# Output mix and up projection on single-bank PSUM tiles, with their sums moved from GpSimd to VectorE

## The chip, the cores and the metric

The kernel runs on one core of a Trainium2 chip. The core has a matmul engine, TensorE (PE in the profile, PEld for its weight loads), and VectorE (DVE), ScalarE (ACT), GpSimd (POOL) and SyncE (SP), each with an instruction queue of its own that it works through in order. SP only issues transfers; POOL issues some too. Matmuls write into PSUM, which has eight banks, and a tile of 128 x 512 float32 fills one bank. The metric is the time of one execution in device microseconds.

## The reference

One decoder block on a sequence of 1024 tokens, width 1024, all in float32:

```python
h = rms_norm(x, pre_norm1_w) * (1 + sc1) + sh1          # sc, sh, g from silu(c) @ w_ada
z, xbc, dt, q, k, v, gates = split(h @ w_in)
y_ssd = ssd_branch(z, xbc, dt, ...)                     # causal conv, state-space scan, gated norm
y_att = diff_attention_branch(q, k, v, ...)             # 8 heads, two softmaxes each, causal
gate_ssd, gate_att = split(sigmoid(gates))
merged = gate_ssd * (y_ssd @ w_ssd_o) + gate_att * (y_att @ w_attn_o)
mix = merged @ w_out
x = x + g1 * rms_norm(mix, post_norm1_w)
h2 = rms_norm(x, pre_norm2_w) * (1 + sc2) + sh2
u_gate, u_val = split(causal_dwconv(h2 @ w_up, conv_ffn_w, conv_ffn_b))   # D_FF = 2816 each
f = (gelu(u_gate) * u_val) @ w_down
x = x + g2 * rms_norm(f, post_norm2_w)
```

## The kernel before

**Numbers.** Every float32 operand is split into a high part (rounded by ScalarE) and a low part (VectorE: operand minus high part), and every product is three matmuls, high-high, high-low and low-high. A unit of work on PE is a 128x128 weight against 128x512. `split` (L88 to L90) is the helper, so all highs have line L89 and most lows L90.

**Stages.** In order: the conditioning rows and h (0 to 75 us from the span's start), the convolved projection xbc with twelve blocks (to 222), z (to 320), v and the state-space scan (to 497), five gate blocks "gs" (to 551), q, k and the scan's output product (to 735), attention (to 1102), its output product "ao" with eight blocks and the merge (to 1194), the passage (the output mix, the second norm, transposes, and the first two pairs of the up projection, to 1361), pairs 2 to 21 of the up projection (to 1764), the down projection (to 1986).

**Who sets the order.** From xbc on, stretches of the program fix the order of some engines by hand, in which an engine's instructions stand as they are written: in the passage and the up projection those of PE, DVE, ACT and POOL. Elsewhere a scheduler orders each queue by what is ready when, as far as it can tell. SP is always the scheduler's.

**The mix.** Eight blocks of 128 tokens; each has a PSUM tile `mix` of two banks (`ps_mm`, two such tiles in all), one bank for each half of the channels. ScalarE squares a half for the norm (`mix_square`, L1361), VectorE scales and adds (`mix_end`), PE transposes the normalized block (`first_half`, `turn`), ScalarE and VectorE make h2's parts from it. A tile is free for the block after next when its squares and scalings are done.

**The up projection** is done by Strassen's rule in Winograd's form. The 1024 rows of h2 make two halves, the tokens two halves, and a pair of channel blocks (a gate block and its value block) is taken together, so a 2x2 by 2x2 block product needs seven products of 12 matmuls each, 84 in all, in place of eight. Their order is in `order`: b11 into bank X, b21 into Z, t2 added into X, t1 into Y, t3 added into X, b22 added into Y, t4 added into X. X and Z are the two halves of one `ps_mm` tile `up`; Y has a bank of its own. Between the products, the bank as it stands is copied out by ScalarE into `evs` (L1653, L1660, L1663), and VectorE adds a bank and a copy (L1657, L1666, L1670) to make the four results `cg` and `cv`. The left operands are weight blocks and four sums of them (`up_sums`, L1269 to L1271), whose splits are made three products ahead; the convolution over tokens of the pair before (`up_conv`: ACT L1317, DVE L1318, ACT L1320, DVE L1322) is spread over the products.

**Sums for the down projection.** It uses the same rule, so it needs sums of the activations `ug` of each second pair (POOL, L1331 to L1334, stored to memory by L1336) and sums of its weights. The latter are made by `down_sums` (L406 to L418), eleven times: POOL loads two blocks of 512 KB into `wdr`, adds and subtracts four times into `wds`, and stores two blocks of 512 KB. Three of these are written into the xbc loop, eight into the z loop; two copies of one column by VectorE (L447) tie the first to block 6 of xbc.

**The first two pairs** are worked together while h2 is being transposed. Their weight sums are made by POOL and VectorE there, as are the sums and differences of h2 (`t2_sum`, `minus_b11`, and POOL's L1555 and L1557).

## Time and profile before

| | |
|---|---|
| Three runs | 1984.0, 1987.07, 1987.69 us; median 1987.07 |
| The profiled execution | 1987.92 us, of which the span is 1986.2 |
| Mean granted TensorE clock | 0.985 |
| Busy PE, DVE, ACT, POOL | 1889.3, 1212.4, 850.6, 310.1 us |
| Data moved by DMA | 301.86 MB, 152 GB/s over the span |

A row of the timeline gives the start in us from the span's start, the duration, the engine, the line, the operation, the tiles written and read, and in square brackets how long the engine stood idle before it and what released it. Matmuls overlap: a row says 0.39 us for a 128x512 matmul, and the next starts 0.23 us later when nothing waits. A row of a group gives the count, the busy time, the mean in ns, and the idle time before. A row of the waits gives the waiting engine and line, the one it waited for, and the total in us, the times and the longest.

### The profile page before, as it was taken

The numbers are of one execution on the slowest core, as the hardware profiler recorded it, in microseconds if no ns is written. First come the engines' busy times: TensorE is split into PE (matmuls) and PEld (weight loads), VectorE is DVE, ScalarE is ACT, GpSimd is POOL, SyncE is SP. The second block draws the span as 40 slices with busy tenths as digits, with TensorE's granted clock in tenths as the row PEclk, the third lists the DMA queues.
The fourth block names the chain that finished last, engine by engine and source line by source line (L and its number), as shares of the span: only waits on it lengthen the run. The fifth ranks groups of instructions, "written<-read, shape, count | busy, mean of one in ns | idle before, by whom it ended". The sixth has DMA issues, their size and how long they took to land.

```text
span 1986.2 us, 24455 instructions
## 1 busy us (share of the span) xinstructions
PE 1889.3 (95%) x9128; PEld 1563.1 (79%) x9128; DVE 1212.4 (61%) x1763; ACT 850.6 (43%) x1634; POOL 310.1 (16%) x282
## 2 busy tenths in 40 slices
PE   6999989999999999999999999888999999999998
PEld 4787988878887788888888787666777777777886
DVE  6967343565254237777766543387878887795545
ACT  5522123555222125665656422454444454555442
POOL 0005551453010000000000000141111211130001
PEclk8999999999999999999999999899999999999999
DMA  9837672133436745665632753111322322277744
GB/s 303 277 116 266 222 238 102 70 106 114 162 91 174 238 144 157 168 191 154 173 114 75 233 174 123 43 43 67 108 90 92 112 100 86 93 251 270 231 156 154
DMA packets 133132, 301.86 MB, mean 152 GB/s; under 512 B 16395, under 2 KB 47755, under 8 KB 133014
## 3 DMA queue, kind: packets, MB, share of 16 engines
q1 hardware_dynamic: 123510, 265.70, 42.2%
q0 software_dynamic: 9504, 34.61, 4.8%
q8 instruction: 72, 1.18, 0.2%
q14 instruction: 46, 0.38, 0.1%
HBM read 213.99 MB, written 86.26 MB: 151 GB/s over the span
## 4 chain that ended last, share of the span: by engine, by line
PE 77%; DVE 9%; DMA 6%; ACT 5%; issue 2%; POOL 1%; SPq 1%; POOLq 0%; DVEq 0%; ACTq 0%
PE up L1293 5%; PE up L1294 4%; PE up L1295 4%; PE o L1074 3%; PE upy L1293 2%; PE upy L1294 2%; PE upy L1295 2%; PE v L608 2%; PE v L609 2%; PE xbc L111 2%; PE v L610 2%; PE xbc L112 1%; PE at L1061 1%; PE xbc L113 1%; PE so L111 1%
## 5 line engine op out<-in xcount | busy, mean ns | idle before, releaser
L1293 PE MATMUL up<-t,wu_t 128*128 128x512 f32 x264 | 107.4, 407 | 21.8 <-ACT evs L1653 17.1
L1294 PE MATMUL up<-t,wu_t 128*128 128x512 f32 x264 | 105.2, 398 | 2.4 <-DVE t L1425 2.4
L1295 PE MATMUL up<-t,wu_t 128*128 128x512 f32 x264 | 104.7, 397 | 0.0
L89 ACT ACTIVATE wu_t<-sab 128x512 fp32r<-128x512 f32 x66 | 39.5, 627 | 126.2 <-DVE sab L1269 118.6
L1062 ACT COPY aT<-at 128x512 f32<-128x512 f32 (+2 forms) x96 | 46.1, 480 | 108.2 <-PE at L1061 108.2
L138 POOL TENSOR_TENSOR sqt<-sqt,nhalf 128x4 f32<-128x4 f32 x16 | 16.1, 1007 | 466.2 <-DVE sqt L137 466.2
L1293 PEld LDWEIGHTS up<-t,wu_t 128*128 128x128 f32 x264 | 50.7, 192 | 41.6 <-ACT evs L1653 25.6
L90 DVE TENSOR_TENSOR g_lo<-gst,g_hi 128x1024 fp32r<-128x1024 f32 (+1 forms) x42 | 48.3, 1157 | 56.3 <-ACT g_hi L89 55.9
L1074 PEld LDWEIGHTS o<-vt,aT 128*128 128x128 f32 x576 | 74.8, 191 | 9.6 <-ACT aT L1062 5.3
L90 DVE TENSOR_TENSOR wu_t<-sab,wu_t 128x512 fp32r<-128x512 f32 x66 | 47.8, 748 | 55.3 <-ACT wu_t L89 55.3
L1074 PE MATMUL o<-vt,aT 128*128 128x128 f32 x576 | 80.9, 276 | 0.2
L89 ACT ACTIVATE g_hi<-gst 128x1024 fp32r<-128x1024 f32 (+1 forms) x42 | 41.3, 989 | 74.0 <-DMA gst<-gld_s 35.7
L1331 POOL TENSOR_TENSOR gsum<-ug,ug 128x512 f32<-128x512 f32 x11 | 17.6, 1597 | 351.5 <-DVE ug L1322 351.5
L111 PE MATMUL xbc<-hT,wx_hi 128*128 128x512 f32 x160 | 64.4, 402 | 4.9 <-DVE cu L441 4.9
L1293 PE MATMUL up<-b,wu_b 128*128 128x512 f32 x176 | 68.6, 390 | 0.0
L1295 PE MATMUL up<-b,wu_b 128*128 128x512 f32 x176 | 68.5, 389 | 0.0
L1294 PE MATMUL up<-b,wu_b 128*128 128x512 f32 x176 | 68.5, 389 | 0.0
L111 PE MATMUL z<-wz_hi,hT 128*128 128x346 f32 (+1 forms) x192 | 63.1, 330 | 4.9 <-ACT wz_hi L89 4.1
L1035 DVE TENSOR_REDUCE nmx<-sc 128x1 f32<-128x640 f32 (+3 forms) x64 | 65.6, 1024 | 2.1
L112 PE MATMUL z<-wz_lo,hT 128*128 128x346 f32 (+1 forms) x192 | 63.2, 329 | 1.6 <-DVE wz_lo L90 1.6
L1356 PE MATMUL mix<-wo_hi,mT 128*128 128x512 f32 x128 | 52.7, 412 | 12.0 <-ACT tm L1361 12.0
L1015 PE MATMUL sc<-kst,qst 128*128 128x512 f32 (+2 forms) x192 | 63.7, 340 | 0.0
(429 smaller groups left out, 5950.4 us busy)
## 6 DMA issues: line engine op xcount, KB each, us to landing
wu_raw<-in_w_up SPq DMA_DIRECT2D x43, 512.0 KB, 3.5
adas<-in_w_ada SPq DMA_DIRECT2D x32, 512.0 KB, 5.0
wdr<-in_w_down POOLq DMA_DIRECT2D x22, 512.0 KB, 6.6
wtd<-wds POOLq DMA_DIRECT2D x22, 512.0 KB, 4.5
gld_s<-gsum POOLq DMA_DIRECT2D x22, 512.0 KB, 3.8
gst<-gld_s SPq DMA_DIRECT2D x20, 512.0 KB, 5.1
wdt_raw<-wtd SPq DMA_DIRECT2D x20, 512.0 KB, 4.3
gld_a<-ug SPq DMA_DIRECT2D x33, 256.0 KB, 2.0
```

Of the source, the lines that this page charges most:

```text
L89: A.activation(hi, raw, AF.Copy)
L90: V.tensor_tensor(lo, raw, hi.bitcast(F32), op=ALU.subtract)
L111: T.matmul(ps, lh, rh, start=(i == 0), stop=False)
L112: T.matmul(ps, lh, rl, start=False, stop=False)
L1015: T.matmul(sc[:, n0:n1], qs_[s][:, tsl], ks_[s][:, n0:n1], start=True, stop=False)
L1035: V.reduce_max(nmx[:, bq, s : s + 1], sc[:, :L], axis=AX.X, negate=True)
L1062: A.copy(at[:, :nk].rearrange("p k q -> p (k q)"), ptr[:, : nk * P])
L1074: T.matmul(po_of[j, grp][:, qi, :], at[:, k, :], vt[j % 2][:, kt, :], start=(kt == 0), stop=(kt == i))
L1293: T.matmul(out_, wh, xh_, start=(k == 0 and first), stop=False, skip_group_check=more)
L1294: T.matmul(out_, wh, xl_, start=False, stop=False, skip_group_check=more)
L1295: T.matmul(out_, wl, xh_, start=False, stop=(k == end), skip_group_check=more)
L1356: T.matmul(o, xh_, wh, start=(k == 0), stop=False)
```

## The change

It has five parts.

1. **PSUM.** The pool of two-bank tiles is closed after attention's output product, and four tiles of one bank each (`ps_m`) take its place. A mix block takes two of them, even blocks 0 and 1, odd blocks 2 and 3; a pair of the up projection takes one for X and one for Z, pairs 0 to 3 as 0/1, 2/3, 1/3, 0/2 and then 1/3 and 0/2 in turn. A mix block's first square is written ahead of the transposes' activations that follow its first part.
2. **POOL to VectorE.** The gate sums are made by VectorE (`up_gsum`), one at a time after four successive products, and stored by SP. The sums and differences of h2 in the passage go to VectorE too.
3. **Early weight sums.** The weight sums of pairs 0, 1 and 2 are written at blocks 0, 1 and 6 of attention's output product (`early_sums`): SP loads the weights, VectorE makes four sums, POOL stores them to memory (`wsd`). The passage loads the finished sums, in the order of the list `loads`. The splits of the first pairs are written in another order, and products 0 and 1 of pair 2 stand ahead of the last product of pairs 0 and 1.
4. **Weight loads.** All raw up weights come through three tiles by `w_load`, called at fixed products.
5. **Down sums.** The two one-column copies go. Six `down_sums` are written into the z loop, five into the gate blocks gs3 to gs7, with tiles taken anew there.

The diff, cut to its core:

```diff
+    pairs_of_banks = ExitStack()
+    pmm = pairs_of_banks.enter_context(tc.tile_pool(name="pmm", bufs=1, space=bass.MemoryType.PSUM))
     def ps_mm(name):
-        return pp.tile([P, 2, HALF], F32, tag="mm", name=name, bufs=2)
+        return pmm.tile([P, 2, HALF], F32, tag="mm", name=name, bufs=2)
...
-            if b == 6:
-                for t_ in wdr:
-                    V.tensor_copy(t_[:, 0, 0:1], u[:, 0:1])
-            if b >= 6 and b % 2 == 0:
-                down_sums(b // 2 - 3)
...
-            if q == 0 or (q == 2 and c0 < 692 and half == 0):
+            if q == 0:
                 down_sums(n_dn)
...
+    wdr = [SL.get(f"wdr{i}", F32, (P, 2, HALF)) for i in range(2)]
+    wds = [SL.get(f"wds{i}", F32, (P, 2, HALF)) for i in range(2)]
     for j in range(3, 8):
+        down_sums(n_dn)
+        n_dn += 1
         w = load_block(a["w_gate"][j], f"wgs{j}")
...
+    def early_sums(m):
+        ra, rb = [wp.tile([P, 2, HALF], F32, tag="wraw", name=f"ws{m}_{i}", bufs=3) for i in range(2)]
+        for r_, b in ((ra, fbs[m]), (rb, NFF + fbs[m])):
+            SP.dma_start(r_.rearrange("p h c -> p (h c)"), a["w_up"][b])
+        a11, a12, a21, a22 = ra[:, 0], ra[:, 1], rb[:, 0], rb[:, 1]
+        V.tensor_tensor(a22, a21, a22, op=ALU.add)
+        V.tensor_tensor(a21, a11, a21, op=ALU.subtract)
+        V.tensor_tensor(a11, a22, a11, op=ALU.subtract)
+        V.tensor_tensor(a12, a12, a11, op=ALU.subtract)
+        for i, (x_, y_) in enumerate(((a11, a22), (a21, a12))):
+            G.dma_start(wsd[m][i][:, 0], x_)
+            G.dma_start(wsd[m][i][:, 1], y_)
...
         w = load_block(a["w_attn_o"][j], f"wao{j}")
+        if j in (0, 1, 6):
+            early_sums(j if j < 2 else 2)
...
+    pairs_of_banks.close()
+    pm = ctx.enter_context(tc.tile_pool(name="pm", bufs=1, space=bass.MemoryType.PSUM))
+    def ps_m(i, name):
+        return pm.tile([P, HALF], F32, tag=f"m{i}", name=name, bufs=1)
...
+    loads = [("f", 0), ("f", 1), ("s", 0), ("s", 1), ("q", 0), ("q", 1), ("a", 0), ("f", 2), ("s", 2), ("q", 2), ("a", 2)]
+    loads += [(n, m) for m in range(3, NPAIR) for n in ("f", "v")]
...
-    def up_banks(fb):
-        mm = ps_mm(f"up{fb}")
-        banks[fb] = {"X": mm[:, 0, :], "Z": mm[:, 1, :]}
+    def up_banks(m, x_, z_):
+        banks[m] = {"X": ps_m(x_, f"upx{m}"), "Z": ps_m(z_, f"upz{m}")}
...
-        G.tensor_tensor(s1, l21, l22, op=ALU.add)
-        G.tensor_tensor(s2, s1, l11, op=ALU.subtract)
-        G.tensor_tensor(s3, l11, l21, op=ALU.subtract)
-        G.tensor_tensor(s4, l12, s2, op=ALU.subtract)
-        for i, n in enumerate(("s12", "s34")):
-            G.dma_start(gld[n][:, k, :, :], gsum[i])
+        o, x_, y_, op = ((s1, l21, l22, ALU.add), (s2, s1, l11, ALU.subtract), (s3, l11, l21, ALU.subtract), (s4, l12, s2, ALU.subtract))[i]
+        V.tensor_tensor(o, x_, y_, op=op)
+        if i % 2:
+            SP.dma_start(gld[("s12", "s34")[i // 2]][:, k, :, :], gsum[i // 2])
...
-        pms[i] = ps_mm(f"mix{i}")
+        pms[i] = [ps_m(2 * (i % 2) + ch, f"mix{i}_{ch}") for ch in range(2)]
...
+                if n == 1:
+                    mix_square(i, 0)
                 if i in (5, 6):
                     for _ in range(1 + (i == 5 and n == 3)):
...
-                if n == 1:
-                    mix_square(i, 0)
...
-        for k in down_k:
-            G.tensor_tensor(part(hb1, k), part(tbs, k), part(hb1, k), op=ALU.subtract)
-        for k in range(KH):
-            G.tensor_tensor(part(hb2, k), part(hb2, k), part(tbs, k), op=ALU.subtract)
...
+                V.tensor_tensor(part(hb1, k - 1), part(tbs, k - 1), part(hb1, k - 1), op=ALU.subtract)
+                high("t3", k - 1, hb1)
...
+        for k in range(KH):
+            V.tensor_tensor(part(hb2, k), part(hb2, k), part(tbs, k), op=ALU.subtract)
...
+        convs = {(m, p): [(up_conv, m - 1, p)] for m in range(3, NPAIR) for p in range(5)}
+        for m in range(4, NPAIR, 2):
+            for i in range(4):
+                convs.setdefault((m + (i == 3), (4 + i) % 7), []).append((up_gsum, m - 1, i))
...
+                up_banks(m, *((0, 2) if m % 2 else (1, 3)))
```

Three places in the order of VectorE's queue. The first is the xbc loop: `cu` is the convolution of a block, `accr` and `adas` belong to the conditioning rows. Before:

```order
L441 SCALAR_TENSOR_TENSOR cu0_818<-xbc6_1125,vec_73,cu0_818 128x1023
L447 COPY wdr0_814<-cu0_818 128x1
L447 COPY wdr1_815<-cu0_818 128x1
L441 SCALAR_TENSOR_TENSOR cu0_818<-xbc6_1125,vec_73,cu0_818 128x1022
L383 SCALAR_TENSOR_TENSOR accr0_806<-adas0_808,scl_79,accr0_806 128x1024
L441 SCALAR_TENSOR_TENSOR cu0_818<-xbc6_1125,vec_73,cu0_818 128x1021
```

The two copies into `wdr`, which POOL's first load of the down weights follows, stand behind block 6's first step. Now:

```order
L445 SCALAR_TENSOR_TENSOR cu0_821<-xbc6_1128,vec_76,cu0_821 128x1023
L387 SCALAR_TENSOR_TENSOR accr0_809<-adas0_811,scl_82,accr0_809 128x1024
L445 SCALAR_TENSOR_TENSOR cu0_821<-xbc6_1128,vec_76,cu0_821 128x1022
L387 SCALAR_TENSOR_TENSOR accr0_809<-adas1_812,scl_82,accr0_809 128x1024
L445 SCALAR_TENSOR_TENSOR cu0_821<-xbc6_1128,vec_76,cu0_821 128x1021
```

They are gone; nothing on this queue stands ahead of those loads.

The second place is the end of attention: `ga7` is the last gate weight, `rsm`, `coef` and `p` are the last softmax step, `sqt` and `osb` the norm of the last heads. Before:

```order
L940 TENSOR_TENSOR ga7_lo_8485<-ga7_raw_8282,ga7_hi_8484 128x512
L1051 RECIPROCAL rsm_5308<-ssum_5306 128x2
L1052 SCALAR_TENSOR_TENSOR coef_5309<-ssum_5306,nlam_5279,rsm_5308 128x1
L1053 SCALAR_TENSOR_TENSOR p1_0_5301<-p1_1_5302,coef_5309,p1_0_5301 128x1024
L1083 TENSOR_TENSOR sqt_5311<-rsm_5308 128x4
L1084 TENSOR_TENSOR sqt_5311<-sqt_5311,sso_5310 128x4
L137 TENSOR_SCALAR sqt_5311<-sqt_5311 128x4
L1092 TENSOR_TENSOR sqt_5311<-sqt_5311,rsm_5308 128x4
L1093 TENSOR_TENSOR osb_5304<-osb_5304,sqt_5311 128x512
```

Now:

```order
L944 TENSOR_TENSOR ga7_lo_8490<-ga7_raw_8287,ga7_hi_8489 128x512
L1216 TENSOR_TENSOR ws0_1_8800<-ws0_1_8800 128x512
L1217 TENSOR_TENSOR ws0_1_8800<-ws0_0_8799,ws0_1_8800 128x512
L1055 RECIPROCAL rsm_5313<-ssum_5311 128x2
L1218 TENSOR_TENSOR ws0_0_8799<-ws0_1_8800,ws0_0_8799 128x512
L1056 SCALAR_TENSOR_TENSOR coef_5314<-ssum_5311,nlam_5284,rsm_5313 128x1
L1219 TENSOR_TENSOR ws0_0_8799<-ws0_0_8799 128x512
L1057 SCALAR_TENSOR_TENSOR p1_0_5306<-p1_1_5307,coef_5314,p1_0_5306 128x1024
L1087 TENSOR_TENSOR sqt_5316<-rsm_5313 128x4
L94 TENSOR_TENSOR wao1_lo_8873<-wao1_raw_8870,wao1_hi_8872 128x1024
L1216 TENSOR_TENSOR ws1_1_8877<-ws1_1_8877 128x512
L1217 TENSOR_TENSOR ws1_1_8877<-ws1_0_8876,ws1_1_8877 128x512
```

The weight sums of pair 0 (`ws0`) stand before and between the three operations of the softmax step; those of pair 1 (`ws1`, with `wao1_lo`) stand in the norm's chain.

The third place is a pair of the up projection whose predecessor closes two pairs: `sab` are the weight sums, `wu` the splits, `ug` the activations. Before:

```order
L1322 TENSOR_TENSOR ug1_10342<-ug1_10342,uv_10343 128x1024
L1666 TENSOR_TENSOR cv0_10208<-up5_11449,evs0_9988 128x512
L1269 TENSOR_TENSOR sab00_9879<-wu38_raw_11564 128x512
L90 TENSOR_TENSOR wu16_b21_11567<-wu16_raw_11537,wu16_b21_11567 128x512
L1670 TENSOR_TENSOR cg0_10207<-upy5_11506,evs0_9988 128x512
L1269 TENSOR_TENSOR sab00_9879<-sab00_9879,wu16_raw_11537 128x512
L90 TENSOR_TENSOR wu16_t2_11584<-sab00_9879,wu16_t2_11584 128x512
L90 TENSOR_TENSOR wu16_t1_11600<-sab00_9879,wu16_t1_11600 128x512
```

Now:

```order
L1366 TENSOR_TENSOR ug1_10456<-ug1_10456,uv_10457 128x1024
L1380 TENSOR_TENSOR gsum0_10458<-ug0_10455,ug1_10456 128x512
L1720 TENSOR_TENSOR cv0_10300<-upx8_11246,evs0_10049 128x512
L1335 TENSOR_TENSOR sab0_10453<-wuv9_11284 128x512
L1322 TENSOR_TENSOR wu9_b21_11360<-wuf9_11191,wu9_b21_11360 128x512
L1380 TENSOR_TENSOR gsum0_10458<-gsum0_10458,ug0_10455 128x512
L1724 TENSOR_TENSOR cg0_10299<-upy8_11306,evs0_10049 128x512
L1335 TENSOR_TENSOR sab0_10453<-sab0_10453,wuf9_11191 128x512
L1322 TENSOR_TENSOR wu9_t2_11379<-sab0_10453,wu9_t2_11379 128x512
L1380 TENSOR_TENSOR gsum1_10459<-ug0_10455 128x512
L1335 TENSOR_TENSOR sab1_10454<-wuf9_11191,sab0_10453 128x512
```

Where the bank sums, weight sums and low parts of a pair followed each other, a gate sum (`gsum`) now stands after each product's own work, four in all; every second pair has them.

446 lines of the change are left out of this document (235 added, 211 removed).

## Prediction

> **What bounds the kernel now.** I read the page's busy shares first, then the busy time by stage, then the waits of the matmul engine (PE), then the timeline around each of its larger waits. A line of the page:
>
> ```profile
> PE 1889.3 (95%) x9128; PEld 1563.1 (79%) x9128; DVE 1212.4 (61%) x1763; ACT 850.6 (43%) x1634; POOL 310.1 (16%) x282
> ```
>
> PE is the bound nearly everywhere, so only what makes PE wait, or slows it, can change the time. Whole stages from the output mix to the steady up projection (columns: window, its length, busy PE, PEld, DVE, ACT, POOL, granted clock, DMA share, GB/s):
>
> ```profile
> 1194.00:1302.00 108.00, 96.00 (x417) 77.49 (x416) 43.43 (x68) 38.13 (x86) 15.29 (x20) 0.95 0.20 75
> 1302.00:1361.00 59.00, 52.18 (x228) 40.58 (x226) 48.47 (x64) 29.15 (x54) 15.81 (x11) 0.94 0.10 37
> 1361.00:1442.00 81.00, 73.70 (x307) 59.16 (x308) 63.89 (x75) 38.73 (x56) 14.03 (x12) 0.96 0.29 101
> 1442.00:1523.00 81.00, 78.30 (x342) 63.55 (x341) 64.39 (x77) 38.62 (x58) 14.72 (x12) 1.00 0.28 98
> ```
>
> The first three lose most, and have the lower clocks. Who is waited for:
>
> ```profile
> ACT evs L1653 <- PE up L1295: 54.5, 18, 3.7
> ...
> PE up L1293 <- ACT evs L1653: 17.1, 20, 4.0
> ...
> PE mix L1356 <- ACT tm L1361: 12.0, 6, 4.9
> ```
>
> The first two rows are a circle: ScalarE's copy of bank X waits for PE, and then PE waits for the copy, once per pair.
>
> **The circle in the up projection.** One round of it, its neighbour 20 us earlier, and the longest:
>
> ```profile
> 1429.42 0.50 PE L1293 MATMUL up<-t,wu_t 128*128 128x512 f32 x1 [0.67 <-ACT evs L1653]
> ...
> 1448.36 0.39 PE L1295 MATMUL up<-b,wu_b 128*128 128x512 f32 x1
> 1448.79 0.58 ACT L1653 COPY evs<-up 128x512 f32<-128x512 f32 x1 [3.71 <-PE up L1295]
> ...
> 1449.42 0.50 PE L1293 MATMUL up<-t,wu_t 128*128 128x512 f32 x1 [0.68 <-ACT evs L1653]
> ...
> 1385.15 1.24 ACT L1317 ACTIVATE ug<-cg,vec 128x1024 f32<-128x1024 f32 x1 [5.54 <-POOL gsum L1333]
> ...
> 1386.91 0.80 PE L1293 MATMUL up<-t,wu_t 128*128 128x512 f32 x1 [4.01 <-ACT evs L1653]
> ```
>
> The copy needs only the first product, in X, but starts when the last matmul of the second, in Z, has ended: X and Z are halves of one tile. A pair takes 1449.42 - 1429.42 = 20.00 us. Its 84 matmuls start 0.2266 apart where nothing waits, 19.03 in all, so the circle costs 0.97 a pair, 18 times: 17.5. The wait of 4.01 has another root, POOL's gate sums in front of ScalarE. Matmuls start 0.43 apart for the next 4.9 us, so that round costs about 6.4. Pairs 2 to 21 hold 1680 matmuls, 380.7 us of 409.0 between their ends, so 28.3 are lost in all; the rest (4.4) are smaller waits in pair 2.
>
> With a tile for each bank, the copy waits for the first product alone, and has the second's 12 x 0.2266 = 2.7 us to be done in: it takes 0.58, behind at most one activation of 1.24 and one weight high part of 0.6, both queued ahead of it on ScalarE. So this wait goes, if VectorE keeps up with its new work. Its rows:
>
> ```profile
> 1372.47 1.28 DVE L1318 SCALAR_TENSOR_TENSOR uv<-cv,vec,uv 128x1023 f32<-128x1023 f32 x1
> ...
> 1373.67 0.68 DVE L1666 TENSOR_TENSOR cv<-up,evs 128x512 f32<-128x512 f32 x1
> 1374.27 0.68 DVE L1269 TENSOR_TENSOR sab<-wu_raw 128x512 f32<-128x512 f32 x1
> 1374.87 0.68 DVE L90 TENSOR_TENSOR wu_b<-wu_raw,wu_b 128x512 fp32r<-128x512 f32 x1
> ...
> 1379.25 1.22 DVE L1322 TENSOR_TENSOR ug<-ug,uv 128x1024 f32<-128x1024 f32 x1
> ...
> L90 DVE TENSOR_TENSOR wu_b<-wu_raw,wu_b 128x512 fp32r<-128x512 f32 x8 | 7.6, 956 | 0.0
> ```
>
> A pair has seven low parts, four weight sums and three bank sums, 14 operations on 128x512, and the four gate sums of every second pair add two: 16. They start 0.60 apart (1373.67, 1374.27, 1374.87) and are busy 0.68 each, so 9.6 to 10.9, with four convolution steps of 1.20 to 1.28 and the product of 1.22: 15.6 to 17.2 us of 19.03. It fits, with 2 to 3 us spare. When the circle is gone, the next to end late is the sum of bank Z and the copy (0.68, behind a low part), which nothing on PE waits for until the pair after next writes that bank; the gate sums' stores move from POOL's queue to SP's, 0.3 us of issue each, behind weight loads whose raw tiles are needed 10 us later: no cost. POOL's gate sums disappear from beside it, and with them the 0.956 mean of the last row (the same operation is 0.68 alone). I take 25.5 of the 28.3; bounds 15 (VectorE late by half a microsecond a pair) and 28.
>
> **The passage.** These rows carry it:
>
> ```profile
> 1194.27 0.69 DVE L1220 SCALAR_TENSOR_TENSOR mt<-gth,ao 128x512 f32<-128x512 f32 x1 [6.05 <-PE ao L113]
> ...
> 1261.81 0.50 PE L1356 MATMUL mix<-wo_hi,mT 128*128 128x512 f32 x1 [3.35 <-ACT tm L1361]
> ...
> 1281.87 0.79 PE L1356 MATMUL mix<-wo_hi,mT 128*128 128x512 f32 x1 [4.94 <-ACT tm L1361]
> ...
> 1311.83 0.30 PE L1418 MATMUL h2tr<-ident,xr 128*128 128x128 f32 x1 [0.89 <-DVE xr L1383]
> ...
> 1332.62 1.75 DVE L1271 TENSOR_TENSOR sab<-wu_raw,sab 128x512 f32<-128x512 f32 x1
> ...
> 1333.93 0.61 PE L1293 MATMUL up<-t,wu_t 128*128 128x512 f32 x1 [2.68 <-ACT t L1422]
> ...
> 1336.23 0.80 PE L1294 MATMUL up<-t,wu_t 128*128 128x512 f32 x1 [1.69 <-DVE t L1425]
> ```
>
> From 1194.07 to 1354.71 PE issues 552 full matmuls (125.1 us) and 64 transposes (0.0875 each, 5.6), so of 160.6 us 30.0 are lost. The mix's waits (12.0, and some 4 of half-rate matmuls after the two long ones) go: a mix block has two tiles of its own out of four, and its first square now stands ahead of the transposes' activations. Of the t waits, the part behind VectorE's 1.75 us weight sums goes, since the sums of pairs 0 to 2 come ready from memory, by five more loads of 512 KB in a stage whose DMA share is 0.20 and 0.10: they are hidden as long as SP issues them a block ahead. VectorE takes over POOL's eight subtractions of the passage, 8 x 0.6 = 5 us, in a window of 59 us where it is busy for 48, part of that being the 1.75 us slowdowns and the sums that go. What stays or is new: the change of pools makes the first mix matmul wait for both gate operations of the last block, 1.3 us from 1194.27 and about 0.4 of hand-over (1.9); the 0.89; lower waits on highs and lows of the third and last products (about 1.0 and 0.6, and 0.7 at the first); the last square, behind a weight load (0.7); transitions I can't place, 2.7. That is 8.5: gain 21.5, bounds 12 and 27.
>
> **The moved sums of the down weights.** They sit on POOL with their own loads, in before from 148 to 296 us without a break:
>
> ```profile
> 85.89 1.21 DVE L90 TENSOR_TENSOR wx_lo<-wx_raw,wx_hi 128x1024 fp32r<-128x1024 f32 x1
> ...
> 172.02 2.38 DVE L383 SCALAR_TENSOR_TENSOR accr<-adas,scl,accr 128x1024 f32<-128x1024 f32 x1 [4.09 <-DMA adas<-in_w_ada]
> ...
> 178.88 1.27 DVE L383 SCALAR_TENSOR_TENSOR accr<-adas,scl,accr 128x1024 f32<-128x1024 f32 x1
> ...
> 183.88 0.77 PE L111 MATMUL xbc<-hT,wx_hi 128*128 128x512 f32 x1 [4.93 <-DVE cu L441]
> ...
> 291.35 0.78 ACT L89 ACTIVATE wz_hi<-wz_raw 128x696 fp32r<-128x696 f32 x1 [5.16 <-DMA wz_raw<-in_w_zdt]
> ...
> 292.19 0.59 PE L111 MATMUL z<-wz_hi,hT 128*128 128x348 f32 x2 [3.66 <-ACT wz_hi L89]
> ...
> 85.00:106.00 21.00, 21.00 (x94) 17.38 (x94) 16.89 (x14) 6.53 (x8) 0.00 (x0) 1.00 0.84 290
> ...
> 120.00:148.00 28.00, 28.00 (x121) 22.50 (x120) 19.68 (x21) 8.59 (x8) 0.00 (x0) 1.00 0.29 94
> ```
>
> The loads of adas and of wz come late while POOL's loads run, and PE stops for 4.93 and 3.66 us, with half-rate matmuls behind each (some 2), and 0.9 at a low part after the second. Without their two one-column copies, six of the eleven sums can start when the tiles they reuse are free, about 75 us, and at the 13.4 us that one takes in before (11 in 148 us) they end near 155; five go to the gate blocks near 500. So both stops lose their rival: 12.0 of about 14, bounds 0 and 14. The new neighbours: from 85 to 106 the DMA engines are at 0.84 already and VectorE is busy for 16.89 of 21 us, with low parts of xbc's weights (85.89) some 2 us ahead of the block at 88 that needs the first of them (+0.5, up to 8, the price of the stop at 183.88); from 120 to 148 they are at 0.29. At 500 POOL's first rotary product queues behind the sums (+0.5, up to 2).
>
> [...]
>
> **The early sums.** Twelve operations of 0.68 and six loads and twelve stores are added at attention's end and in its output product. Those of pair 2 run beside output products; VectorE has 47 us of work in those 92 (1102 to 1194), so 2.7 more are free there. Those of pairs 0 and 1 stand, in the built order, inside the last softmax step and the last norm:
>
> ```profile
> 1082.63 0.30 PE L1061 MATMUL at<-ident,p 128*128 128x128 f32 x1 [0.95 <-DVE sqt L1083]
> ...
> 1093.77 0.32 SPq L1162 DMA_DIRECT2D stg<-atd  x1
> ...
> 1107.27 0.63 ACT L89 ACTIVATE oT<-stg 128x512 fp32r<-128x512 f32 x1 [2.31 <-DMA stg<-atd]
> ...
> 1102.00:1194.00 92.00, 89.41 (x386) 71.64 (x385) 47.11 (x66) 25.81 (x36) 0.00 (x0) 1.00 0.60 201
> ```
>
> PE already waits 0.95 for the probabilities, and two sums between reciprocal and product add 1 to 1.4. SP's stg loads stand behind weight loads that now wait for POOL's stores of the sums; at about 1097 instead of 1093.77 they make the first output products wait 2 to 3, where one already lands late (2.31). Taken: 4.5, bounds 1 and 9.
>
> **The sum**, against the profiled execution's 1987.92 us: -25.5 -21.5 -12.0 +0.5 +0.5 +4.5 = -53.5, so 1934.4. The shown median is 0.85 below that execution: 1933.6. I say **1934**.
>
> **The rivals.**
> VectorE late in each pair by half a microsecond, because its queue is in order and a low part stands behind bank sums that wait for PE: 20 x 0.5 = 10, 1944. For it: 82 to 91% busy; against: weights are prepared three products ahead. Chance 0.15.
> The hand-over at attention's end costs 14.5 instead of 4.5 (the loads late, then half-rate matmuls): 1944. Chance 0.13.
> [...] Chance 0.09.
> The copy still waits for the second product, so that only the 4.01 round and smaller waits go: 17.5 back, 1951. The separate tiles speak against it. Chance 0.03.
> On the other side, VectorE sets the pace of the up projection. Sixteen operations at the slowed row's 0.956 with the rest at 6.35 are 21.6 us a pair; with 0.4 of waits 22.0, and 20 x (22.0 - 19.03) = 59: 1993. It decides from 21.7 us a pair on (53.5 / 20 above 19.03). Against it: the slowing came from POOL, which leaves. Chance 0.06, 0.02 of it within 0.2% of before (about what a measurement of this kernel tells from no change).
> **My forecast** has 0.54: its own range is 1925 to 1943. The range of 8 in 10 reaches over the first three rivals, 1923 to 1954. So faster by over 0.2%: 0.94; within: 0.02; slower: 0.04.
>
> **What would show it.** Right: no row of PE waiting for the copy of X; pairs 19.0 to 19.3 us apart; the mix's row on the squares gone; POOL idle from 155 to 330 and no stop near 184 and 292; a new wait of about 1.9 at the first mix matmul. Wrong: pairs at 19.5 or more with a VectorE row as releaser; stops of xbc before 120; several waits of the first output products on DMA.

## The result and the profile after

The changed kernel takes **1937.87 us** (median of four runs, 1935.66 to 1939.14); the kernel before, run beside it, 1985.53 (1981.89 to 1987.69). The ratio is **0.9761**, with a 95% interval of 0.9742 to 0.9779. The profiled execution took 1938.42, its span 1936.6 us.

First the page's busy time, then rows of the list of PE's waits behind the start (what waits, for what; us in total, times, longest):

```profile
PE 1871.4 (97%) x9128; PEld 1557.7 (80%) x9128; DVE 1204.9 (62%) x1819; ACT 852.2 (44%) x1634; POOL 212.2 (11%) x214
```

```profile
PE dx L1814 <- DVE wdb_lo L94: 5.1, 1, 5.1
PE xbc L115 <- DVE cu L445: 4.8, 2, 3.6
PE upx L1344 <- ACT evs L1712: 4.8, 2, 3.5
...
PE at L1065 <- DVE sqt L1087: 2.1, 1, 2.1
...
PE mix L1402 <- DVE mt L1244: 1.5, 1, 1.5
```

The wait for the copy of X behind the first product (L1653), 20 times in before, is gone altogether. The two waits left on ScalarE's copies are for the other copy of X, the one after t1 (L1712, in before L1660, where PE waited for it once, 1.1 us); both stand in the first pairs. The wait for the squares (12.0) is gone. The longest of these waits now stands in the down projection, where no cost was expected. No row on z's weights is left. The windows (the same columns as before: window, length, busy PE, PEld, DVE, ACT, POOL, clock, DMA share, GB/s) for the mix, the first two pairs, pairs 2 to 5, steady pairs, and the start of the down projection:

```profile
1185.80:1277.30 91.50, 91.19 (x417) 75.30 (x417) 39.22 (x68) 37.35 (x86) 7.61 (x14) 1.00 0.22 79
1277.30:1337.00 59.70, 54.42 (x249) 43.35 (x247) 42.88 (x66) 32.11 (x56) 1.47 (x2) 1.00 0.26 88
1337.00:1418.00 81.00, 77.97 (x335) 64.05 (x336) 71.28 (x92) 42.88 (x63) 0.00 (x0) 0.98 0.29 101
1418.00:1499.00 81.00, 81.00 (x359) 67.07 (x358) 68.01 (x90) 39.68 (x59) 0.00 (x0) 1.00 0.31 107
1712.00:1793.00 81.00, 75.92 (x326) 62.14 (x325) 52.89 (x54) 40.99 (x51) 0.00 (x0) 0.96 0.77 258
```

In steady pairs PE is busy for the whole window: 359 matmuls in 81 us, where before had 342. One round there, from the timeline, with the same copy a pair earlier:

```profile
1448.36 0.59 ACT L1703 COPY evs<-upx 128x512 f32<-128x512 f32 x1 [0.99 <-PE upx L1346]
...
1467.20 0.39 PE L1344 MATMUL upz<-b,wu_b 128*128 128x512 f32 x1
...
1467.40 0.59 ACT L1703 COPY evs<-upx 128x512 f32<-128x512 f32 x1 [0.26 <-PE upx L1346]
```

The copy of X starts 0.2 us after Z's first matmul, not after Z's last one, and the copies stand 19.04 apart.

Where the time went, by stage, from the first matmul of each stage in the profiled executions (two experiments that are told below stand beside the two kernels; v, scan and gates reach from the last matmul of z to that of the gates, the next two stages from last matmul on):

| stage, us | before | after | banks alone | best version |
|---|---|---|---|---|
| start to z | 221.29 | 221.01 | 221.15 | 214.78 |
| z | 102.17 | 92.17 | 99.92 | 92.13 |
| v, scan, gates | 232.08 | 230.79 | 231.08 | 229.47 |
| q, k, scan's output product | 163.04 | 163.37 | 163.05 | 166.45 |
| attention | 383.65 | 385.70 | 383.49 | 383.49 |
| attention's output product | 91.84 | 92.81 | 93.14 | 88.86 |
| mix | 108.23 | 91.45 | 91.44 | 91.39 |
| up projection | 461.37 | 434.70 | 443.19 | 436.83 |
| down projection, to the end | 222.53 | 224.60 | 221.64 | 221.9 |

### The profile page after: what moved, and what is told of

It reads as the page before. It is cut to its first block, busy times and chain, and to the rows that moved or that the text cites. A ratio compares the mean times of both kernels' runs of the same rounds, so it can differ in the third digit from the quotient of the medians.

```text
span 1936.6 us, 24512 instructions
## 1 busy us (share of the span) xinstructions
PE 1871.4 (97%) x9128; PEld 1557.7 (80%) x9128; DVE 1204.9 (62%) x1819; ACT 852.2 (44%) x1634; POOL 212.2 (11%) x214
## 3 DMA queue, kind: packets, MB, share of 16 engines
q8 instruction: 72, 1.18, 0.3%
## 4 chain that ended last, share of the span: by engine, by line
PE 78%; DVE 10%; DMA 5%; ACT 4%; issue 3%; SPq 1%; POOL 0%; POOLq 0%; DVEq 0%; ACTq 0%
PE upx L1345 3%; PE upx L1346 3%; PE upx L1344 3%; PE o L1078 3%; PE dx L1814 2%; PE dx L1815 2%; PE dx L1813 2%; PE upy L1345 2%; PE upy L1346 2%; PE upy L1344 2%; PE v L606 2%; PE v L607 2%; PE dy L1815 2%; PE dy L1813 2%; PE z L116 2%
## 5 line engine op out<-in xcount | busy, mean ns | idle before, releaser
L1344 PE MATMUL upx<-t,wu_t 128*128 128x512 f32 x264 | 104.0, 394 | 4.8 <-ACT evs L1712 4.8
L1345 PE MATMUL upx<-t,wu_t 128*128 128x512 f32 x264 | 103.7, 393 | 1.9 <-DVE t L1459 1.9
L1346 PE MATMUL upx<-t,wu_t 128*128 128x512 f32 x264 | 103.2, 391 | 0.0
L1318 ACT ACTIVATE wu_t<-sab 128x512 fp32r<-128x512 f32 x57 | 34.0, 626 | 122.5 <-DVE sab L1335 122.5
L142 POOL TENSOR_TENSOR rsf<-rsf,nhalf 128x1 f32<-128x1 f32 x8 | 5.6, 703 | 639.6 <-DVE rsf L141 636.9
L115 PE MATMUL xbc<-hT,wx_hi 128*128 128x512 f32 x160 | 64.4, 402 | 4.8 <-DVE cu L445 4.8
L1344 PEld LDWEIGHTS upx<-t,wu_t 128*128 128x128 f32 x264 | 49.9, 189 | 16.6 <-ACT evs L1712 5.6
L1020 PE MATMUL sc<-klo,qst 128*128 128x512 f32 (+2 forms) x192 | 63.2, 346 | 0.0
L116 PE MATMUL xbc<-hT,wx_hi 128*128 128x512 f32 x160 | 63.0, 394 | 0.0
L117 PE MATMUL xbc<-hT,wx_lo 128*128 128x512 f32 x160 | 62.8, 393 | 0.0
L115 PE MATMUL z<-wz_hi,hT 128*128 128x346 f32 (+1 forms) x192 | 61.8, 324 | 0.0
L117 PE MATMUL z<-wz_hi,hT 128*128 128x346 f32 (+1 forms) x192 | 61.5, 320 | 0.0
L1345 PEld LDWEIGHTS upx<-t,wu_t 128*128 128x128 f32 x264 | 50.0, 189 | 13.2 <-DVE t L1459 2.9
```

Source lines behind the costliest of these rows:

```text
L115: T.matmul(ps, lh, rh, start=(i == 0), stop=False)
L116: T.matmul(ps, lh, rl, start=False, stop=False)
L117: T.matmul(ps, ll, rh, start=False, stop=(i == n - 1))
L1020: T.matmul(sc[:, n0:n1], qs_[s][:, tsl], kl[s][:, n0:n1], start=False, stop=True)
L1344: T.matmul(out_, wh, xh_, start=(k == 0 and first), stop=False, skip_group_check=not first)
L1345: T.matmul(out_, wh, xl_, start=False, stop=False, skip_group_check=not first)
```

## The experiments

Each is an edit of the changed kernel, timed beside the kernel before. Medians are compared with the changed kernel's 1937.87, whose four executions reach from 1935.66 to 1939.14; the kernel before had medians of 1985.31, 1984.75 and 1984.95 beside them. So a difference of medians under some 3 us shows little by itself. A stage is compared by one profiled execution of each kernel.

**The copy waits for Z again.** One column of Z is copied out by ScalarE ahead of the copy of X, from pair 3 on, so that the wait of before comes back while the tiles stay apart.

```diff
                 elif p == 1:
+                    if m > 2:
+                        A.copy(jk, bank["Z"][:, 0:1])
                     A.copy(ev_of(m, 0), bank["X"])
```

> The changed kernel, but from pair 3 on ScalarE reads one column of bank Z before it copies bank X, so that the copy waits again for the last matmul of the second product; nothing else differs, and the tiles stay one bank each. Theory (the copy's wait was the circle that cost 0.97 us a pair): 19 pairs go from 19.03 back to 20.0 to 20.3 us (the extra read takes about 0.2), so 18 to 24 us over the change, about 1958. Rival (the gain of the up projection comes from POOL having left VectorE's side, or from the new order of the weight splits): less than 5 us over the change, about 1940, pairs at 19.1 to 19.3.

Measured: 1956.26 us, ratio 0.9851 (0.9836 to 0.9866), 18.4 above the change. A row of its waits:

```profile
PE upx L1344 <- ACT evs L1706: 14.0, 19, 0.7
```

Nineteen waits of 0.74, and pairs 20.09 apart instead of 19.04: 19 x 1.05 = 20.0, and the up projection takes 454.6 instead of 434.7. So the circle is the wait that the forecast named, and its price is about what a pair was said to lose (0.97; the 1.05 has the added read in it).

**The banks alone.** The kernel before with nothing but the first part of the change, for the mix, the up projection and the down projection's four `dy` tiles; the sums stay on POOL, no early sums, the down sums and the squares where they were.

```diff
+    pairs_of_banks.close()
+    pm = ctx.enter_context(tc.tile_pool(name="pm", bufs=1, space=bass.MemoryType.PSUM))
...
-        mm = ps_mm(f"up{fb}")
-        banks[fb] = {"X": mm[:, 0, :], "Z": mm[:, 1, :]}
+        q = 2 * (fbs.index(fb) % 2)
+        banks[fb] = {"X": ps_m(q, f"upx{fb}"), "Z": ps_m(q + 1, f"upz{fb}")}
...
-        pms[i] = ps_mm(f"mix{i}")
+        pms[i] = [ps_m(2 * (i % 2) + ch, f"mix{i}_{ch}") for ch in range(2)]
```

> The kernel before with the first part of the change alone: the tiles of the mix, of X and Z and of the down projection's second bank group are of one bank each (a mix block and a pair take banks 0 and 1 or 2 and 3 in turn). All sums stay where they were. Theory: the copy's circle goes (0.97 us in 18 pairs), less 0.25 a pair for VectorE slowed by POOL, as the run with the gate sums on POOL shows: 12 to 16 in the up projection; the mix's waits on the squares go in part, 4 to 10; 16 to 26 us below before, about 1964. Rival (single banks help only together with the sums' move): less than 8 us below before.

Measured: 1949.75 us, ratio 0.9832 (0.9795 to 0.9869), 35.0 below the kernel before: more than I expected. The windows of its first pairs, of pairs 2 to 5 and of steady pairs:

```profile
1283.30:1343.00 59.70, 51.87 (x226) 40.65 (x225) 49.99 (x64) 29.40 (x54) 17.36 (x12) 0.94 0.11 36
1343.00:1424.00 81.00, 75.85 (x326) 61.95 (x326) 66.81 (x79) 41.24 (x60) 14.05 (x12) 0.98 0.29 101
1424.00:1505.00 81.00, 81.00 (x359) 67.05 (x358) 68.36 (x83) 41.38 (x61) 14.72 (x12) 1.00 0.30 104
```

The last row has POOL at 14.72 us, its gate sums in their old place, and still 359 matmuls in 81 us. The mix takes 91.44, as in the change, with its squares in their old order. So the banks alone give all of the mix's gain and all of the steady pairs' gain. What parts 2 to 4 bring in the up projection is 443.19 - 434.70 = 8.5: 3.2 in pairs 0 to 2, 4.4 in pair 3 (25.02 against 20.67, where PE still waits 4.05 for a copy), 0.9 in the last pair, and nothing between, where all pairs stand 19.04 apart in both kernels. How the 3.2 divides between the early sums, the loads and the sums taken from POOL was not tried.

**The gate sums back on POOL**, at the places that the change gives them:

```diff
-        V.tensor_tensor(o, x_, y_, op=op)
+        G.tensor_tensor(o, x_, y_, op=op)
         if i % 2:
-            SP.dma_start(gld[("s12", "s34")[i // 2]][:, k, :, :], gsum[i // 2])
+            G.dma_start(gld[("s12", "s34")[i // 2]][:, k, :, :], gsum[i // 2])
```

> The changed kernel with the gate sums of the up projection on POOL again (four operations every second pair, stores on POOL's queue), at the same places in the program. Theory (PE waited for the copy, not for VectorE, and VectorE has 2 to 3 us in hand either way): within 3 us of the change, pairs at 19.0 to 19.2, VectorE's low parts beside POOL slowed to 1.7 us as before, in the shade of PE. Rival (POOL beside VectorE was part of the loss): 5 to 15 us slower than the change.

Measured: 1942.62 us, ratio 0.9788 (0.9772 to 0.9805), 4.75 above the change, between what the theory allowed and what the rival asked for. The up projection takes 445.4, 10.7 more: 0.6 in pairs 0 to 2; 3.3 in pair 3, where a wait of 3.04 at 1362.74 stands in place of one of 1.30; 4.0 in eight later pairs, every second one being 19.53 long; 2.8 in the last pair, with waits of 1.34 and 0.33. So pairs are not at 19.0 to 19.2 throughout, as the theory had it. The down projection takes 218.2 (6.4 less). Groups of VectorE's work from 1380 to 1540 us, first in the change, then with the sums on POOL:

```profile
L1322 DVE TENSOR_TENSOR wu_b<-wuf,wu_b 128x512 fp32r<-128x512 f32 x18 | 12.3, 686 | 4.5 <-ACT wu_b L1318 4.5
...
L1335 DVE TENSOR_TENSOR sab<-sab,wuf 128x512 f32<-128x512 f32 x9 | 6.1, 681 | 0.0
L1335 DVE TENSOR_TENSOR sab<-wuv 128x512 f32<-128x512 f32 x9 | 6.1, 680 | 0.0
```

```profile
L1322 DVE TENSOR_TENSOR wu_b<-wuf,wu_b 128x512 fp32r<-128x512 f32 x17 | 16.0, 943 | 4.4 <-ACT wu_b L1318 4.4
L1335 DVE TENSOR_TENSOR sab<-sab,wuf 128x512 f32<-128x512 f32 x8 | 14.9, 1857 | 0.0
...
L1335 DVE TENSOR_TENSOR sab<-wuv 128x512 f32<-128x512 f32 x8 | 8.4, 1044 | 0.0
```

The same operations take 1857, 1044 and 943 ns beside POOL's sums, and 681, 680 and 686 without: 8 x 1.176 + 8 x 0.364 + 17 x 0.257 = 16.7 us more in the 160. In the change VectorE's eighteen gate sums of that window take 12.3 us. VectorE is busy for less time when it does the sums itself: 136.3 us of the 160 against 138.8. At the places of before it is not so: with the banks alone, POOL doing the sums there, VectorE is busy for 133.8 in the same window, and no pair in it is longer than 19.04.

The largest rise, 1.18 an operation, is nearly as long as one of POOL's operations in that window (1.28 to 1.62).

**The last pair's gate sums on POOL**, all others on VectorE:

```diff
-        V.tensor_tensor(o, x_, y_, op=op)
+        last = m == NPAIR - 1
+        (G if last else V).tensor_tensor(o, x_, y_, op=op)
         if i % 2:
-            SP.dma_start(gld[("s12", "s34")[i // 2]][:, k, :, :], gsum[i // 2])
+            (G if last else SP).dma_start(gld[("s12", "s34")[i // 2]][:, k, :, :], gsum[i // 2])
```

> The changed kernel with the gate sums of the last pair alone on POOL again. In the change's profile the first down product waits 5.08 us for a weight's low part on VectorE, with half-rate matmuls behind it, and the stage from the first down matmul to the end takes 224.6 us, against 222.5 before and 218.2 in the run with all gate sums on POOL. Theory (VectorE's last four sums stand ahead of that low part): the wait falls under 1 us and the stage to about 218.5; 5 to 6 us below the change. Rival (that weight's load is late for reasons of SP's queue): the wait stays at 3 to 5 us, within 2 us of the change.

Measured: 1936.94 us, ratio 0.9768 (0.9736 to 0.9801), no difference. The down projection's first waits:

```profile
1726.59 0.50 PE L1815 MATMUL dx<-wdb_lo,g_hi 128*128 128x512 f32 x1 [0.93 <-DVE wdb_lo L94]
...
1733.33 0.50 PE L1815 MATMUL dx<-wdb_lo,g_hi 128*128 128x512 f32 x1 [0.96 <-DVE wdb_lo L94]
...
1791.27 0.50 PE L1815 MATMUL dx<-wdt_lo,g_hi 128*128 128x512 f32 x1 [3.20 <-DVE wdt_lo L94]
```

The first wait falls from 5.08 to 0.93, so VectorE's sums were its cause, as the theory said, and the rival's wait of 3 to 5 us did not come. But the price was not there to gain: other waits come, at 1733.33 and 1791.27, the three add up to 5.09, as much as the one before, and the stage takes 225.0 against 224.6. The stall moves on, which neither case had foreseen. In the two later kernels that have this edit among others these waits add up to 2.7 and 3.5 and the stage takes 221.0 and 221.9; with the wait of the first experiment put back, which leaves these sums on VectorE, it takes 221.5. One execution each doesn't settle what the edit is worth.

**The down sums as before**, three in xbc, eight in z:

```diff
+            if b == 6:
+                for t_ in wdr:
+                    V.tensor_copy(t_[:, 0, 0:1], u[:, 0:1])
+            if b >= 6 and b % 2 == 0:
+                down_sums(b // 2 - 3)
...
-            if q == 0:
+            if q == 0 or (q == 2 and c0 < 692 and half == 0):
                 down_sums(n_dn)
...
-        down_sums(n_dn)
-        n_dn += 1
         w = load_block(a["w_gate"][j], f"wgs{j}")
```

> The changed kernel with the eleven sums of the down weights where they were: three in the xbc loop behind the one-column copies, eight in the z loop, none beside the gate blocks. Theory (POOL's loads delayed z's weights): the stop of 3.7 us near 292 us and the half-rate matmuls behind it come back in the z stage, 9 to 12 us over the change, about 1948; the xbc stage ends where it does in both kernels, since both had a stop near 184. Rival (the z stage gained by something else, the order of its loads): within 3 us of the change.

Measured: 1947.28 us, ratio 0.9804 (0.9788 to 0.982), 9.4 above the change. Both stops are there:

```profile
184.65 0.76 PE L115 MATMUL xbc<-hT,wx_hi 128*128 128x512 f32 x1 [5.29 <-DVE cu L445]
...
291.94 0.66 PE L115 MATMUL z<-wz_hi,hT 128*128 128x348 f32 x1 [3.50 <-ACT wz_hi L93]
```

So the move is worth 9.4, of which z has 7.6 (99.73 against 92.17). The stop near 184 is in the change too:

```profile
152.83 1.07 POOL L414 DMA_DIRECT2D wdr<-in_w_down  x2
160.20 1.29 POOL L417 TENSOR_TENSOR wds<-wdr 128x512 f32<-128x512 f32 x1 [6.31 <-DMA wdr<-in_w_down]
...
166.94 1.12 POOL L422 DMA_DIRECT2D wtd<-wds  x2
...
175.06 1.29 DVE L387 SCALAR_TENSOR_TENSOR accr<-adas,scl,accr 128x1024 f32<-128x1024 f32 x1 [3.02 <-DMA adas<-in_w_ada]
...
183.59 0.47 PE L115 MATMUL xbc<-hT,wx_hi 128*128 128x512 f32 x1 [3.65 <-DVE cu L445]
```

The sixth sum is not ready at 155: its loads are issued at 152.83, land at 160.2, and its stores go out at 166.94, so it still runs beside the loads of adas, on which VectorE waits until 175.06.

The first wait of xbc in the change, near 111, is not in before:

```profile
104.57 2.31 DVE L94 TENSOR_TENSOR wx_lo<-wx_raw,wx_hi 128x1024 fp32r<-128x1024 f32 x1
...
110.86 0.47 PE L115 MATMUL xbc<-hT,wx_hi 128*128 128x512 f32 x1 [1.17 <-DVE cu L445]
```

The low part at 104.57 runs beside one of POOL's sums, which takes 2.28 from 105.76 on. In the run with the early weight sums later, whose program is the same up to here, this low part takes 1.22, and PE does not stop. The eight profiled executions with this part of the program have this stop at 0 to 2.03 us, seven of them over 0.5.

**All six early down sums at z's start.** Two one-column copies from the tenth block of xbc hold the first sum back:

```diff
             if q == 0:
+                if n_dn == 0:
+                    for t_ in wdr:
+                        V.tensor_copy(t_[:, 0, 0:1], xbcT[10][:, 0:1])
                 down_sums(n_dn)
```

> The changed kernel with the first six of the down weights' sums held back, by two one-column copies, until the xbc stage is over, so that they run in the z stage; five stay beside the gate blocks. POOL then works nowhere in the xbc stage. Theory (the stop of xbc near 184 us, 1.4 to 5.3 us in the five profiles so far, comes from POOL's loads and stores beside the loads of the conditioning rows): the stop falls below 1 us and xbc ends near 203 in place of 208.6; the z stage takes a stop back, 0 to 5 us; in sum 5 below the change to 2 above. Rival (the conditioning rows' own loads and those of z's weights fill the transfers by themselves): the stop stays at 2 to 5 us, and the time is 0 to 6 over the change.

Measured: 1939.26 us, ratio 0.9784 (0.9752 to 0.9816), no difference. In its trace xbc's products end 6.7 earlier, with no stop, and z takes 98.2 instead of 92.2, with this wait and two of 0.7:

```profile
PE z L115 <- ACT wz_hi L93: 2.5, 1, 2.5
```

With POOL's sums in xbc PE stops there for 3.65 (the change), with them in z for 2.5 there (this run): moving the sums moved the stop.

**The down sums split**: the condition of the last edit with `n_dn == 4` in place of 0, so four run early, two at z's start, five in the gate blocks.

> Only the split of the down sums: four in their early place, two held back until the first gate products of z, five where they were. Theory that the stop near 184 comes of more of GpSimd's transfers than the early stretch has room for: no stop near 184, end of xbc 6.7 earlier as where all six were moved, and z unchanged at 92.2 since two sums are a third of the load: 1931. Rival that any sum at z's start delays the loads of z's weights: z 2 to 6 longer, 1933 to 1938.

Measured: 1934.52 us (1931.74 to 1938.62), ratio 0.9753 (0.9729 to 0.9777), 3.4 below the change, with ranges that overlap: the time alone falls into the rival's 1933 to 1938 and decides little. In its trace the first z product comes 7.0 earlier than in the change (213.99 against 221.01), z takes 92.14, and no wait of xbc or z on these weights is left. So z did not grow, as the rival had it: two sums fit between 198 and 223, where the six did not. The profiled execution is 4.9 shorter, 1931.7: later stages took 2.1 back (the scan's output product 0.4, the up projection 1.3, the down projection 0.5).

**The early weight sums later**, at blocks 3, 5 and 6 of attention's output product:

```diff
-        if j in (0, 1, 6):
-            early_sums(j if j < 2 else 2)
+        if j in (3, 5, 6):
+            early_sums((3, 5, 6).index(j))
```

> The changed kernel with the early weight sums written at blocks 3, 5 and 6 of attention's output product in place of 0, 1 and 6, so that they no longer stand in the last softmax step and the last norm. Theory (they cost 2 us at attention's end): the wait of 2.12 us for the last probabilities falls to about 1 and attention's output product starts 1.5 to 2.5 us earlier; 1 to 3 us below the change, about 1936. Rival (the hand-over is set by the loads of the attention output, and the sums only fill a gap): within 0.7 us of the change, or slower, if the later sums delay the passage's loads.

Measured: 1933.74 us (1931.55 to 1938.01), ratio 0.9742 (0.9724 to 0.976), 4.1 below the change. Attention takes 383.41 instead of 385.70, its output product 91.09 instead of 92.81: 4.0 together. Why, is to be seen in the change, in the last softmax step:

```profile
1068.99 0.16 DVE L1055 RECIPROCAL rsm<-ssum 128x2 f32<-128x2 f32 x1
1069.10 0.69 DVE L1218 TENSOR_TENSOR ws<-ws,ws 128x512 f32<-128x512 f32 x1
1069.71 0.21 DVE L1056 SCALAR_TENSOR_TENSOR coef<-ssum,nlam,rsm 128x1 f32<-128x1 f32 x1
1069.85 0.68 DVE L1219 TENSOR_TENSOR ws<-ws 128x512 f32<-128x512 f32 x1
1070.45 1.28 DVE L1057 SCALAR_TENSOR_TENSOR p<-p,coef,p 128x1024 f32<-128x1024 f32 x1
...
1071.87 0.30 PE L1065 MATMUL at<-ident,p 128*128 128x128 f32 x1 [2.12 <-DVE sqt L1087]
```

Two weight sums stand between the reciprocal and the product that PE waits for. Without them that wait is 0.95, as in before.

**Three repairs together**: the early sums later, the last pair's gate sums on POOL, and in pair 2 the bank's copies ahead of the first pair's convolution at one product more.

```diff
-                if m == 2 and p in (3, 4):
+                if m == 2 and p == 4:
                     for f_, *x_ in todo:
                         f_(*x_)
```

> The changed kernel with three edits: the early weight sums at blocks 3, 5 and 6; in pair 2 ScalarE copies bank X after the fourth product ahead of the activations of pair 0's convolution (the change's profile has PE waiting 3.48 us for that copy at 1338.72, behind two activations, a table load and a gelu); the gate sums of the last pair on POOL. Theory: 2 to 3, 4 to 6 and 5 to 6 us: 11 to 15 below the change, 1923 to 1927. Rival (the stall in pair 2 moves to the next product, and the last one is a late load): 3 to 6 below the change.

Measured: 1931.15 us (1929.2 to 1932.28), ratio 0.9737 (0.9707 to 0.9766), 6.7 below the change, just over the rival's 3 to 6 and far from the theory's 11 to 15; the first repair alone gave 4.1. The down projection takes 221.0, 3.6 less; the up projection only 0.9 less, since the wait of 3.48 in pair 2 became one of the next product:

```profile
1338.89 0.50 PE L1344 MATMUL upy<-b,wu_b 128*128 128x512 f32 x1 [3.58 <-ACT evs L1718]
```

**The first pair's convolution one product later**, all copies ahead of it:

```diff
-            (2, 2): ((0, 0), (0, 1)),
-            (2, 3): ((0, 2), (0, 3)),
-            (2, 4): ((0, 4),),
-            (2, 5): ((1, 0),),
+            (2, 2): (),
+            (2, 3): ((0, 0), (0, 1)),
+            (2, 4): ((0, 2), (0, 3)),
+            (2, 5): ((0, 4), (1, 0)),
...
-                if m == 2 and p in (3, 4):
-                    for f_, *x_ in todo:
-                        f_(*x_)
-                    todo = []
```

> Only the order in the first pairs' up projection: the first pair's convolution starts one product later and stands behind the copies that give banks back. Theory that the stops at 1338 and 1345 (3.48 and about 1) come of the convolution's ScalarE steps ahead of the copy: the wait on ACT's evs falls below 0.5 there, pair 2 takes 27 instead of 30.4: 1933 to 1935. Rival that the ScalarE steps with their table load hit the next copy instead: pair 2 and 3 together within 1 of before, 1937 to 1938.

Measured: 1942.7 us (1939.22 to 1943.73), ratio 0.9789 (0.9768 to 0.9811), 4.8 above the change. The up projection is 1.6 longer, pairs 2 and 3 together 52.0 against 51.1; the other 3 us lie elsewhere in the trace, 1.6 of them in xbc. The theory falls: the one long wait becomes three.

```profile
1342.02 0.50 PE L1344 MATMUL upy<-b,wu_b 128*128 128x512 f32 x1 [1.03 <-ACT evs L1713]
...
1347.11 0.79 PE L1344 MATMUL upx<-t,wu_t 128*128 128x512 f32 x1 [2.08 <-DVE cv L1716]
...
1364.94 0.50 PE L1344 MATMUL upx<-t,wu_t 128*128 128x512 f32 x1 [2.16 <-ACT evs L1708]
```

What is queued there in the change, on ScalarE:

```profile
1335.85 1.28 ACT L1364 ACT_TABLE_LOAD   x1 [1.58 <-DVE ug L1362]
1337.14 1.06 ACT L1364 ACTIVATE ug<-ug 128x1024 f32<-128x1024 f32 x1
1338.11 0.57 ACT L1712 COPY evs<-upx 128x512 f32<-128x512 f32 x1
```

Three convolutions have to fit into the time of two pairs here, with a table load in the first; no order of them that was tried freed PE.

**The single-bank pool opened ahead of attention's output product**, whose blocks then use two such tiles each:

```diff
+    pairs_of_banks.close()
+    pm = ctx.enter_context(tc.tile_pool(name="pm", bufs=1, space=bass.MemoryType.PSUM))
...
     for j in range(8):
...
-        ps = ps_mm(f"ao{j}")
+        ps = [ps_m(2 * (j % 2) + half, f"ao{j}_{half}") for half in range(2)]
```

> Only the place of the pool's switch: the single-bank tiles are opened ahead of the output product, which then uses them for its sums. Theory that the 1.47 at the first matmul of the passage is the switch: it vanishes, and each half of an output tile comes free by itself: 1.5 to 2.5 less, 1935.5 to 1936.5. Rival that the switch costs the same at the output product's start, where the last attention tiles are read out: 1937.5 to 1939.

Measured: 1939.86 us (1934.99 to 1942.18), ratio 0.9771 (0.9742 to 0.9799): the whole shows nothing. In its trace the wait of 1.47 at the mix's first matmul is gone, and the output product takes 91.14 instead of 92.81, so the step itself gives 1.7, within the 1.5 to 2.5 expected. Its profiled execution is 3.3 longer than the change's all the same, since q, k and the scan's output take 167.7 instead of 163.4, with a stop where the instructions stand in the same order in both kernels:

```profile
577.71 2.36 POOL L850 TENSOR_TENSOR qf<-qf,ropc 128x1024 f32<-128x1024 f32 x1 [6.20 <-DVE sw L849]
578.14 3.02 DVE L851 TENSOR_TENSOR sw<-sw,rops 128x1024 f32<-128x1024 f32 x1
...
581.87 1.11 PE L822 MATMUL ytr<-ident,yr 128*128 128x128 f32 x4 [2.83 <-DVE yT L825]
```

VectorE's product, which began behind POOL's, takes 3.02. Where it begins ahead, in the change some 19 us earlier, it takes 1.20, and POOL's operation is the long one:

```profile
559.18 1.20 DVE L851 TENSOR_TENSOR sw<-sw,rops 128x1024 f32<-128x1024 f32 x1
559.60 1.94 POOL L417 TENSOR_TENSOR wds<-wdr 128x512 f32<-128x512 f32 x1 [4.43 <-DMA wdr<-in_w_down]
```

In the change the product at this place takes 3.03 too, but the chain begins 2.6 us earlier, and PE does not wait there.

**The best version**: the split, the early sums later, the pool opened earlier, the last pair's gate sums on POOL, and the later convolution.

> All five repairs together: early weight sums begun after attention's end, the down sums split (four early, two at the start of z's products, five in the gate sums' stage), the first pair's convolution one product later with the bank's copies ahead of it, the single-bank pool opened ahead of the output product, the last pair's lows and sums on GpSimd. Theory that each removed stall is net time: 2.5 (attention's end) + 6.7 (xbc's stop) + 3 to 5 (first pairs) + 1.5 (pool's switch) = 14 to 16 below the change, 1922 to 1924. Rival that stalls only move along, as the copies ahead of the convolution did: only attention's end and the switch stay, 1931 to 1934.

Measured: **1926.9 us** (1925.13 to 1927.81), ratio **0.9712** (0.9692 to 0.9732), 11.0 below the change and 58 below the kernel before, between the theory's 1922 to 1924 and the rival's 1931 to 1934. (The expectation names the last pair's lows as well; the edit moves the sums alone.) By the table of stages: xbc 6.2 less, v to gates 1.3, attention 2.2, its output product 4.0, the down projection 2.7; against that 3.1 more at the scan's output and 2.1 more in the up projection, since the later convolution is in it, which by itself had cost time. The 3.1 are the stop of the last experiment again:

```profile
574.75 0.66 PE L825 MATMUL ytr<-ident,yr 128*128 128x128 f32 x4 [2.90 <-DVE yT L828]
```

POOL's first rotary product stands behind the eleventh down sum and starts 25.6 us after the gates' end, in the change 22.5: here the term for q and k, 0.5 and up to 2 in the prediction, is 3. In the last experiment, whose sums stand as in the change, it starts 25.3 after the gates' end; in the nine other kernels with five sums at the gates 20.6 to 22.5, and none of them has the stop. What makes it late in these two executions was not found. A version without the later convolution and with one down sum less at the gates was not tried.

## Why the prediction was right, point by point

The forecast was 1934, the time 1937.87, 3.9 more and inside the range. By its terms, from the profiled executions:

| term | forecast | measured |
|---|---|---|
| pairs 2 to 21 of the up projection | -25.5 | -21.2 |
| passage | -21.5 | -20.7 |
| down sums, with +0.5 and +0.5 | -11.0 | -11.2 |
| early sums | +4.5 | +1.4 |
| down projection | 0 | +2.1 |
| sum | -53.5 | -49.6 |

- **The circle** was right, in its cause and in its price. From pair 4 on, all pairs stand 19.04 apart (forecast 19.03), and the wait put back cost 18.4 us. VectorE is not late there: its rival (1944) did not come. It was mis-sized in the first pairs: 7.0 us are lost from 1334 to 1375, where 2.8 were left over in the sum. What I took for smaller waits is a stop of 3.48, with about 1.7 of half-rate matmuls behind it, and one of 1.30. At the first, the first pair's convolution with its table load stands ahead of the copy of X on ScalarE. The second is an effect of the change that the forecast put at nothing: the four gate sums of the first two pairs stand together on VectorE, the activation that overwrites the `ug` they read waits for them on ScalarE, and the copy stands behind the activation:

```profile
1359.18 1.24 ACT L1361 ACTIVATE ug<-cg,vec 128x1024 f32<-128x1024 f32 x1 [2.17 <-DVE gsum L1380]
```

So the root of before's 4.01 is still there, smaller. The forecast counted ScalarE's rows at steady pairs only.
- **The passage** was right: 9.3 are left of 30.0, 8.5 were forecast. The switch of pools costs 1.5 of waiting (1.9 forecast). What the prediction gave to two causes in the mix (own tiles, the first square moved ahead) is the tiles' alone: the banks alone bring the mix to 91.44. The early sums and VectorE's part give 8.5 in the up projection, but the banks alone, set beside the run with the down sums as before, show what they cost elsewhere: 0.7 at attention's end, 2.1 at its output product, 3.3 in the down projection. Parts 2 to 4 of the change together are worth 1949.75 - 1947.28 = 2.5 us by the medians, of some 48, and that is within what the executions scatter. It was hidden in the sum, since that went by stages and not by parts.
- **The down sums** came out at the forecast's number by luck, by two errors against each other. z gave 10.0, and not 6.6: it lost its long wait with the half-rate matmuls, and smaller waits (on low parts, and on `ev`, into which a block of z is copied out) with it. Some 2 of the 10.0 are chance: the banks alone, with before's program there, take 99.92. The stop near 184 gave nothing: the failed step is the end of the six sums "near 155". They took from 75 to 168, 15.5 each, and not the 13.4 of before, a rate from a stretch with more room on the DMA engines (their busy share is 0.72 from 148 to 296 in before, 0.80 from 75 to 168 here). Two of the prediction's own signs went against it: the stop near 184 stayed, and xbc has a stop before 120, the one of 1.17 at 110.86, for which the sum had 0.5.
- **The early sums**: in the last softmax step the two sums between reciprocal and product cost 1.17, as worked out (1 to 1.4). The output product waits 1.12 and 0.52 for its operands, where 2 to 3 on top of before's were forecast; before had 1.07 and 0.73 there (the 2.31 in the prediction's row is ScalarE's idle time, not PE's). So the late loads were mis-sized: they cost nothing. Against later places the whole cost is 4.0, since those places also shorten the output product below before's.
- **The down projection** was not in the sum. VectorE makes the last pair's gate sums in front of a low part, and PE waits 5.08; the prediction counts the gate sums among VectorE's work in steady pairs, where they are free, and has no price for the last pair, which has no pair behind it to hide them. Before had one wait of 3.06 in this stage, at another weight. Moving these sums to POOL moved the wait, and the stage took 225.0 alone and 221.0 and 221.9 with other edits; what the queue's order is worth of the 2.1 stays open.
- **The rivals.** The others did not come either: attention's hand-over cost 1.4 against before and not 14.5, the moved sums gained, the copy doesn't wait, and VectorE, at 68 of 81 us, doesn't set the pace. The chance of 0.09 was for moved sums that gain nothing and cost 5 us in their new place (1950), an estimate of the author's, and no run shows such a cost. VectorE's slowed operations did reach PE in the 40 us from 75 on: the stop at 110.86 stands behind a low part that took 2.31 beside POOL's sum. But that stop is 1.17.
